# The output map of a SwiGLU feed-forward in three float32r passes, turned to token-major with one Strassen level

## The chip, the cores and the metric

The kernel runs on one core of one Trainium2 chip. The metric is the device time of one execution in microseconds, the median of three runs. The traces come from the hardware profiler.

## What is computed

One layer of a streaming encoder over 1024 prompt tokens and 64 sample tokens, 1024 channels wide: a mixer (stick-breaking attention, spatial gating and cross-attention in parallel), then a feed-forward of 2816 inner channels. The change lies in the last line:

```python
def rmsnorm(x, g):
    y = x * lax.rsqrt(jnp.mean(x * x, axis=-1, keepdims=True) + EPS)
    return y * g

def ffn_sublayer(x, g_pre, w_ffn_in, w_ffn_out, g_post):   # w_ffn_in [1024, 5632], w_ffn_out [2816, 1024]
    a, b = jnp.split(rmsnorm(x, g_pre) @ w_ffn_in, 2, axis=-1)
    return x + rmsnorm((jax.nn.silu(a) * b) @ w_ffn_out, g_post)
```

All of it is float32.

## The kernel before, in words

**Numbers.** A float32 operand is split into two float32r tiles, hi (a rounded copy, by ACT or by a CAST on DVE) and lo (source minus hi, a TENSOR_TENSOR on DVE); `split` chooses the engine of hi with `lighter`, which compares estimated clocks. A product is three passes, hi·hi, hi·lo and lo·hi (`mm3`).

**Layout.** Activations lie transposed, channels on partitions; the 1088 tokens are two halves of 544, each of sub-blocks of 288 and 256 columns. `ffn_in_unit` computes 128 inner channels with one Strassen–Winograd level (`strassen_unit`), applies silu and the gate, and stores the rows to DRAM, `actS[f]`, of which there are 22.

**The feed-forward output.** `fout_pair` calls `conv_pair` for a group of 6, 6, 5 or 5 channel blocks (`FGROUPS`) and two column tiles of 128 output channels: the weights (`whl`) are the stationary operand, the activations (`acth`, `actl`, loaded and split once by `load_act`) move, 288 or 256 columns a matmul. That is the ordinary product: 22 blocks of the contraction, 8 column tiles, three passes, 1088 columns. The sums of the groups are added up in `yacc`. The last group runs in three column groups of 512, 320 and 256 tokens (`GROUPS`), so that one group's tail runs beside the next one's products.

**The tail.** `ffn_tail` squares the rows on ACT (`ysq`), sums them over partitions with a ones-matmul, takes 1 / rms by a pow on GpSimd, transposes the 128x128 fp32 blocks back to tokens on TensorE (`pt<-ident,yacc`), and `post_stages` scales and adds the residual (SCALAR_TENSOR_TENSOR `o<-pt,rst,x2r`) before the store.

**Order.** Python emits the instructions. `run` takes the steps of products in order; `get_wop` makes weight operands `LA` steps ahead and loads `RA` further; everything else stands in streams of stages that `fill` and `breathe` take when the estimated clocks say so. Each engine then runs its own queue in that order. Loads and stores all go through SP's queue.

All instructions are recorded by one helper, so every row of the trace has line 73 (L73); tiles tell them apart.

Of the kernel before, what the change touches and what calls it, by code (L numbers as in the profile page):

```python
# [28 lines left out]
FGROUPS = [6, 6, 5, 5]  # L29
# [19 lines left out]
LA_END = 4  # L49
LA_BR = 4  # L50
# [8 lines left out]
# estimates of instructions, in us, which only order the emission: fixed part, per element of a partition  # L59
# [3 lines left out]
class Engine:  # L63
    """An engine of nc that also advances the estimated clocks."""
# [18 lines left out]
class Clocks:  # L83
    """Estimated time at which each engine has done what was emitted, and at which tiles are written and read."""
# [60 lines left out]
def encoder_layer(  # L145
# [125 lines left out]
    x2sc = [dtile([P, D], f"x2sc{t}") for t in range(9)]  # L271
    actS = [dtile([P, T], f"actS{f}") for f in range(22)]
# [45 lines left out]
    def ready(t):  # L318
        """the first stream whose next stage can start by t, or the one that can start first before t"""
# [17 lines left out]
    def breathe():  # L337
        """background stages that can start, between two short runs of products"""
# [7 lines left out]
    def fill(t):  # L346
        """background stages while products wait until t"""
# [48 lines left out]
    def wop(fn, *rs):  # L396
        """an operand made by fn from the raws rs"""
# [17 lines left out]
    def raw_load(srcs, nk):  # L415
        """srcs: one [nk*128, 256] block, or two of [nk*128, 128]"""
# [21 lines left out]
    # column ranges of the sub-blocks inside a two-bank PSUM tile; together they are contiguous  # L438
# [157 lines left out]
    def tile_rows(i):  # L596
        """token runs of token tile i: tiles 2j, 2j+1 hold the same columns of the two halves; tile 8 both rests"""
# [15 lines left out]
    def nrows(i):  # L613
        return P if i < 8 else 64
# [229 lines left out]
    def transposed(c, fin):  # L844
        """c: [128 ch, T] -> token-major [128, 9, 128]; block 8 holds the sample tokens on partitions 64.."""
# [73 lines left out]
    def load_o(b, t, s, gate=lambda: True):  # L919
        """streams that load and split the operands of branch b from the rows of the half t, sub-block s"""  # L920
# [82 lines left out]
    def post_stages(i, cols_y, rst, res_load, d, gate):  # L1003
        """d["o"] = row tile i scaled by rst(), plus the residual d["x"]; cols_y(): column blocks of its transpose"""
# [21 lines left out]
    def tile_cols(Y, i, c, pad_n=2):  # L1026
        """columns of token tile i, and their tiles, inside the tiles Y[q] ([P, 8 / len(Y), 2, n], first column c of each half)"""
# [9 lines left out]
    def row_stats(tiles, sq, c, R):  # L1037
        """1 / rms of the token tiles, one column each, from the sums sq of squares ([P, 2, n]) per partition, into R"""
# [27 lines left out]
    def mix_tail(js, Y, sq, c):  # L1066
# [4 lines left out]
        for n, i in enumerate(tiles):  # L1071
# [5 lines left out]
            def keep_x2(i=i, d=d):  # L1077
                later(0, lambda o=d["o"]: store(x2sc[i][:nrows(i)], o), [d["o"]])
# [52 lines left out]
    def ffn_in_unit(f, phases):  # L1131
# [14 lines left out]
    ACT = {}  # L1146

    def load_act(f, gate=lambda: True):
        d = {}

        def ld():
            d["r"] = A([P, T], F32, "actr")
            load(d["r"], actS[f])

        def sp():
            hi, lo = A([P, T], F32R, "acth"), A([P, T], F32R, "actl")
            split(d.pop("r"), hi, lo)
            ACT[f] = (hi, lo)
        stream(("sync", lambda: 0 if gate() else None, ld), ("act", lambda: at(d["r"]), sp))

    f0 = 0
    fgs = []
    for ng in FGROUPS:
        fgs.append(list(range(f0, f0 + ng)))
        f0 += ng

    def fout_pair(gi, p, g):
        fs = fgs[gi]
        n0 = (len(fs) + 1) // 2
# [12 lines left out]
        def evac(m_, hi, pt):
            m = 2 * p + m_
            if g is None:
                if gi == 0 and hi == 0:
# [665 lines left out]
```

## Time and profile before

| | before |
|---|---|
| median of 3 runs | 2359.42 us (2359.52, 2355.78, 2359.42) |
| the profiled execution, its own time | 2359.5 us |
| span in that profile | 2359.5 us |
| feed-forward output, first matmul to the end | 2066.2 to 2359.5 us |
| PE, DVE, ACT, POOL busy | 96%, 66%, 32%, 7% |
| matmul instructions | 17,531 |

PE is TensorE, PEld its weight loads, DVE VectorE, ACT ScalarE, POOL GpSimd, SP the engine whose queue issues the transfers. A row of the timeline has a start, a duration, engine, line, operation, tiles (out<-in) and shape; two or more operations of one kind in a row share a row (x2), and square brackets give the idle time before it and what ended it. A matmul row's duration contains its passage through the array, so the time that one takes from its neighbours is read from start to start. PEclk or the granted clock is a share of 2.4 GHz.

### The profile page before, as it was taken

The numbers are of one execution on the slowest core, as the hardware profiler recorded it, in microseconds if no ns is written. First come the engines' busy times: TensorE is split into PE (matmuls) and PEld (weight loads), VectorE is DVE, ScalarE is ACT, GpSimd is POOL, SyncE is SP. The second block draws the span as 40 slices with busy tenths as digits, with TensorE's granted clock in tenths as the row PEclk, the third lists the DMA queues.
The fourth block names the chain that finished last, engine by engine and source line by source line (L and its number), as shares of the span: only waits on it lengthen the run. The fifth ranks groups of instructions, "written<-read, shape, count | busy, mean of one in ns | idle before, by whom it ended". The sixth has DMA issues, their size and how long they took to land.

```text
span 2359.5 us, 42390 instructions
## 1 busy us (share of the span) xinstructions
PE 2270.7 (96%) x17531; PEld 2231.4 (95%) x17531; DVE 1559.2 (66%) x2408; ACT 752.6 (32%) x1325; POOL 154.2 (7%) x246
## 2 busy tenths in 40 slices
PE   7899999999999999988899999988999999999998
PEld 6799999999999998877899999988999999999997
DVE  7856688867786665799824345397667666743357
ACT  8432223232222224776512122343111211221223
POOL 1000000000000000334100000220000000000012
PEclk9999999999999999999999999998999999999998
DMA  6532356755583237754435342332222222432235
GB/s 202 179 102 99 123 206 218 237 185 179 197 269 111 93 131 269 275 194 159 141 120 159 106 155 82 123 110 64 65 74 83 83 77 62 142 120 83 93 113 172
DMA packets 239700, 333.50 MB, mean 141 GB/s; under 512 B 12100, under 2 KB 195988, under 8 KB 239508
## 3 DMA queue, kind: packets, MB, share of 16 engines
q1 hardware_dynamic: 239508, 330.78, 41.9%
q8 instruction: 139, 2.28, 0.4%
q14 instruction: 53, 0.43, 0.1%
HBM read 218.60 MB, written 112.13 MB: 140 GB/s over the span
## 4 chain that ended last, share of the span: by engine, by line
PE 47%; DVE 3%; issue 1%; DMA 0%; ACT 0%; POOLq 0%; POOL 0%; DVEq 0%; ACTq 0%
PE pb L73 46%; PE pt L73 1%; DVE whl L73 1%; DVE bt L73 0%; DMA raw<-in_w_ffn_out_dram 0%; DVE o L73 0%; DVE XhT2a L73 0%; DVE t L73 0%; DVE XhT2b L73 0%; DVE XlT3a L73 0%; DVE XlB11a L73 0%; DVE yacc L73 0%; DVE u L73 0%; DVE XhT1a L73 0%; DVE XlT2a L73 0%
## 5 line engine op out<-in xcount | busy, mean ns | idle before, releaser
L73 ACT ACTIVATE whl<-raw 128x512 fp32r<-128x512 f32 (+2 forms) x319 | 186.9, 604 | 513.0 <-PE pb L73 174.5
L73 DVE TENSOR_TENSOR c<-pb,u 128x544 f32<-128x544 f32 (+2 forms) x236 | 168.3, 713 | 246.1 <-PE pb L73 233.7
L73 PE MATMUL pb<-acth,whl 128*128 128x256 f32 (+3 forms) x1328 | 267.1, 298 | 0.6 <-DVE whl L73 0.4
L73 DVE TENSOR_TENSOR whl<-raw,whl 128x512 fp32r<-128x512 f32 (+1 forms) x382 | 239.6, 645 | 12.1 <-ACT whl L73 9.3
L73 PEld LDWEIGHTS pb<-acth,whl 128*128 128x128 f32 x1328 | 214.3, 190 | 4.9 <-DVE whl L73 1.4
L73 PE MATMUL pb<-actl,whl 128*128 128x256 f32 (+3 forms) x664 | 197.4, 297 | 0.0
L73 DVE TENSOR_TENSOR u<-pb,u 128x544 f32<-128x544 f32 (+2 forms) x177 | 125.8, 711 | 85.6 <-PE pb L73 85.6
L73 DVE TENSOR_TENSOR whl<-u,whl 128x512 fp32r<-128x512 f32 x232 | 160.0, 690 | 6.0
L73 PE MATMUL pb<-XhB11a,whl 128*128 128x288 f32 x656 | 145.0, 297 | 1.2 <-ACT whl L73 1.0
L73 PE MATMUL pb<-XhB21a,whl 128*128 128x288 f32 x656 | 145.0, 297 | 0.0
L73 PE MATMUL pb<-XhB22a,whl 128*128 128x288 f32 x656 | 144.2, 295 | 0.0
L73 PE MATMUL pb<-XhB11b,whl 128*128 128x256 f32 x656 | 132.7, 285 | 0.0
L73 PE MATMUL pb<-XhB21b,whl 128*128 128x256 f32 x656 | 131.6, 284 | 0.0
L73 PE MATMUL pb<-XhB22b,whl 128*128 128x256 f32 x656 | 131.1, 283 | 0.0
L73 PEld LDWEIGHTS pb<-actl,whl 128*128 128x128 f32 x664 | 126.5, 190 | 1.7
L73 ACT ACTIVATE c<-c 128x1088 f32<-128x1088 f32 x38 | 42.4, 1115 | 263.2 <-DVE c L73 263.2
L73 PEld LDWEIGHTS pb<-XhB11a,whl 128*128 128x128 f32 x656 | 109.8, 188 | 1.6 <-ACT whl L73 1.2
L73 PEld LDWEIGHTS pb<-XhB22a,whl 128*128 128x128 f32 x656 | 109.8, 188 | 0.0
L73 PEld LDWEIGHTS pb<-XhB21a,whl 128*128 128x128 f32 x656 | 109.8, 188 | 0.0
L73 PE MATMUL pb<-Xrh,whl 128*128 128x288 f32 (+1 forms) x512 | 102.1, 295 | 6.9 <-DVE whl L73 6.9
L73 PEld LDWEIGHTS pb<-XhB11b,whl 128*128 128x128 f32 x656 | 108.2, 192 | 0.1
L73 PEld LDWEIGHTS pb<-XhB22b,whl 128*128 128x128 f32 x656 | 107.6, 191 | 0.0
(306 smaller groups left out, 6416.3 us busy)
## 6 DMA issues: line engine op xcount, KB each, us to landing
raw<-in_w_in_dram SPq DMA_DIRECT2D x72, 512.0 KB
raw<-in_w_ffn_in_dram SPq DMA_DIRECT2D x88, 256.0 KB
gsc<-c SPq DMA_DIRECT2D x24, 544.0 KB
grow<-gsc SPq DMA_DIRECT2D x24, 544.0 KB
raw<-in_w_branch_dram SPq DMA_DIRECT2D x24, 512.0 KB
raw<-in_w_ffn_out_dram SPq DMA_DIRECT2D x32, 384.0 KB
actS<-c SPq DMA_DIRECT2D x22, 544.0 KB
actr<-actS SPq DMA_DIRECT2D x22, 544.0 KB
```

Source lines behind the costliest of these rows:

```text
L73: r = fn(*a, **k)
```

## The change

The output map is computed token-major: the split activations (`fop`, 128 channels by 128 tokens) are stationary, and 512 columns of the split weights move. One Strassen–Winograd level goes over the halves of the contraction (11 blocks each), of the 1024 prompt tokens and of the 1024 output columns. Seven products p1, p2, p6, p7, p5, p3, p4 in that order take 11 steps each; a step is one channel block, with 2 token pairs (`jp`) of 2 tiles, 3 passes, 12 matmuls of 512 columns.

- **Operands** (`fout_ops`). Weight tiles `fw` of 128x512 are loaded for each product anew. p6 loads three, makes T1 = B12 - B11 on GpSimd (`psub`) and T2 = B22 - T1 on DVE and stores both to DRAM (`tS`), from which p5 and p4 load them again. p7's difference of weights is on DVE, p4's on GpSimd. Activations are loaded as `fa`, 44 half rows, from the last units of ffn_in on (`fout_load`, `FA_GATE`), and stay; the sums S1 are made on GpSimd (`padd`), the differences on DVE (p6) or GpSimd (p7, p3). Each operand is then split.
- **Sample tokens** (64) ride in p1, p2, p5 and p3 as two more matmuls a step whose stationary operand holds hi and lo side by side (`fs`); two fp32 matmuls with `sel` add the halves at the end. They are the ordinary product.
- **Sums of products** (`fout_post`): two-bank PSUM tiles of 128x1024 go into `t1`, `C11`, `U3`, `C22` in SBUF, by ACT or DVE. `scaled` squares with a running sum on ACT (no ones-matmul, no transposes) and multiplies by the gain: on GpSimd for C11 and C22, on DVE else.
- **p4** runs first its 11 steps for the first two token tiles only and keeps the operands (`first`), then the other two tiles one after the other with nothing to make (`rest`).
- **End:** `square` takes 1 / rms by token and one SCALAR_TENSOR_TENSOR a half row adds the residual, then half rows are stored, 18 in all.
- Lookahead in the stage: `LA_END` 4 operands as before, `RA_END` 2 for loads. Ahead of the stage, `x2sc` is stored by token, and each of the 22 units stores its 64 sample columns apart (32 KB more on SP's queue).

```diff
-ACT = {}
-def load_act(f, ...): ...
-def fout_pair(gi, p, g): ...        # conv_pair over FGROUPS, yacc, ysq
-def ffn_tail(js, sq, c): ...        # row_stats, transposes, post_stages
...
+            def put():
+                store(actS[f], c[0][:, :1024])
+                store(sS[f // 11][:, f % 11], c[0][:, 1024:])
+                STORED.add(f)
...
+    def fout_ops(name, k):
+        B = {"11": lambda: w_raw(k, 0), "12": lambda: w_raw(k, 512), "21": lambda: w_raw(NK + k, 0),
+             "22": lambda: w_raw(NK + k, 512)}
+        r = [x() for x in {"p1": [B["11"]], "p2": [B["21"]], "p6": [B["12"], B["11"], B["22"]],
+                           "p7": [B["22"], B["12"]], "p5": [lambda: t_raw(0, k)], "p3": [B["22"]],
+                           "p4": [B["21"], lambda: t_raw(1, k)]}[name]]
+        def w():
+            x = [get_raw(i) for i in r]
+            if name == "p6":
+                psub(x[0], x[0], x[1])
+                sub(x[2], x[2], x[0])
+                later(0, lambda: store(tS[0][k], x[0]), [x[0]])
+                later(0, lambda: store(tS[1][k], x[2]), [x[2]])
+                return fsplit(x[2])
+            if name == "p7":
+                sub(x[0], x[0], x[1])
+            elif name == "p4":
+                psub(x[0], x[0], x[1])
+            return fsplit(x[0])
+        def a():
...
+            if name in ("p1", "p2", "p4", "p5"):
+                return fsplit(src(*{"p1": (0, 0), "p2": (0, 1), "p4": (1, 1), "p5": (1, 0)}[name]))
+            if name == "p6":
+                until(lambda: ("s1", k // 2) in FO)
+                x = src(0, 0)
+                sub(x, src(1, 0), x)
+                return fsplit(x)
+            if name == "p7":
+                x = U([P, 512], F32, "fs3")
+                psub(x, src(1, 1), src(0, 0))
+                return fsplit(x)
+            x = src(0, 1)
+            psub(x, x, src(0, 0))
+            return fsplit(x)
+        return wop(w, *r), wop(a)
...
+    def fout_mm(pt, a, w, jp, js, k):
+        for j in js:
+            mm3(pt[:, (j % 2) * 512:(j % 2) * 512 + 512], a[:, 0, j * P:(j + 1) * P], a[:, 1, j * P:(j + 1) * P],
+                w[:, 0], w[:, 1], k == 0, k == NK - 1)
...
+    def scaled(j0, m, c, eng):
+        for i in range(2):
+            square(j0 + i, m, c[:, i])
+        g = FO["g"][:, m * 512:(m + 1) * 512]
+        for i in range(2):
+            eng(c[:, i], c[:, i], g)
...
+    def fout_post(name, jp, pt):
...
+        if name == "p1":
+            act(new("t1"), src)
+        elif name == "p2":
+            c = new("C11")
+            add(c, src, FO["t1", jp])
+            scaled(2 * jp, 0, c, pmul)
+        elif name == "p6":
+            t = FO["t1", jp]
+            add(t, src, t)
+        elif name == "p7":
+            add(new("U3"), src, FO["t1", jp])
+        elif name == "p5":
+            c = new("C22")
+            add(c, src, FO["U3", jp])
+            t = FO["t1", jp]
+            add(t, src, t)
+            scaled(4 + 2 * jp, 1, c, pmul)
+        elif name == "p3":
+            t = FO.pop(("t1", jp))
+            add(t, src, t)
+            scaled(2 * jp, 1, t, mul)
...
-    for n, f in enumerate(fgs[0]):
-        load_act(f, lambda n=n: pos[0] > p1 + n)
+    fout_load(p1)
     run(7)
     LA[0] = LA_END
-    drain()
+    RA[0] = RA_END
+    fout_begin()
     run(n_fout)
     drain()
```

Two places in the order of the instructions. The first is GpSimd's queue where p2 ends and p6 begins. Before, it held at the end of the program the last sums of squares (`ysq`):

```order
L73 TENSOR_TENSOR ysq_24784<-ysq_24784,ysq_24812 128x512
L73 TENSOR_TENSOR ysq_24784<-ysq_24784,ysq_24841 128x512
L73 TENSOR_TENSOR ysq_24784<-ysq_24784,ysq_24870 128x512
L73 TENSOR_TENSOR ysq_24784<-ysq_24784,ysq_24899 128x512
```

Now (`fa` a sum S1, `fw` the weight differences of p6's steps, `C_` the gain products of C11):

```order
L73 TENSOR_TENSOR fa_22895<-fa_22895,fa_22765 128x1024
L73 TENSOR_TENSOR fw_23258<-fw_23258,fw_23260 128x512
L73 TENSOR_TENSOR fw_23284<-fw_23284,fw_23286 128x512
L73 TENSOR_TENSOR C_3075_23336<-C_3075_23336,gpf_22800 128x512 x2
L73 TENSOR_TENSOR C_3080_23354<-C_3080_23354,gpf_22800 128x512 x2
L73 TENSOR_TENSOR fw_23315<-fw_23315,fw_23317 128x512
L73 TENSOR_TENSOR fw_23368<-fw_23368,fw_23370 128x512
```

The differences of steps 0 and 1 stand ahead of the four products, that of step 2 behind them.

The second is DVE's queue in the same place. Before, in the early part of the stage, it held one lo of 384 columns for several matmuls, and copies into `yacc`:

```order
L73 COPY yacc_22867<-pb_22869 128x544
L73 TENSOR_TENSOR whl_22911<-raw_22738,whl_22911 128x384
L73 TENSOR_TENSOR whl_22916<-raw_22820,whl_22916 128x384
L73 TENSOR_TENSOR actl_22932<-actr_22929,acth_22931 128x1088
L73 COPY yacc_22962<-pb_22919 128x544
```

Now, from C11's additions to the operands of p6's step 2 (`pb` is a PSUM tile of products, `t_` is t1, `ys` the sample rows):

```order
L73 TENSOR_TENSOR C_3075_23336<-pb_23087,t_3030_23065 128x1024
L73 TENSOR_TENSOR C_3080_23354<-pb_23094,t_3031_23073 128x1024
L73 TENSOR_TENSOR ys_3085_23366<-pt_23101,ys_23077 128x512
L73 TENSOR_TENSOR fw_23319<-fw_23319,fw_23315 128x512
L73 CAST fop_23376<-fw_23319 128x512
L73 TENSOR_TENSOR fop_23376<-fw_23319,fop_23376 128x512
L73 TENSOR_TENSOR fa_22526<-fa_22870,fa_22526 128x512
L73 CAST fop_23380<-fa_22526 128x512
```

All operations of an operand of p6 stand on DVE, its first behind a GpSimd difference (`fw_23315`).

## Rows read from the trace of the kernel before

**Rows 1.** From the page: the span; busy time and instructions of PE, and the granted clock in 40 equal slices (tenths).

```profile
span 2359.5 us, 42390 instructions
...
PE 2270.7 (96%) x17531; PEld 2231.4 (95%) x17531; DVE 1559.2 (66%) x2408; ACT 752.6 (32%) x1325; POOL 154.2 (7%) x246
...
PEclk9999999999999999999999999998999999999998
```

**Rows 2.** The tile `acth` on PE, hi activations of the feed-forward output: minimum, median and maximum duration in ns, first and last start, forms.

```profile
L73 PE MATMUL pb<-acth,whl x1328: 274/293/562, 2066.2 to 2348.0; 128*128 128x256 f32 x89, 128*128 128x288 f32 x78, 128*128 128x320 f32 x12, 128*128 128x512 f32 x11
```

**Rows 3.** Stretches: length, then busy us and instructions of PE, PEld, DVE, ACT, POOL, granted clock, DMA share, GB/s. The first lies at the end of ffn_in, the others in the feed-forward output.

```profile
2050.00:2060.00 10.00, 10.00 (x82) 10.00 (x82) 8.44 (x13) 4.51 (x6) 0.00 (x0) 1.00 1.00 365
2100.00:2150.00 50.00, 50.00 (x400) 50.00 (x399) 17.65 (x27) 9.97 (x16) 0.00 (x0) 1.00 0.28 90
2310.00:2320.00 10.00, 10.00 (x73) 9.73 (x72) 9.36 (x18) 4.55 (x11) 2.91 (x3) 1.00 0.91 317
```

**Rows 4.** Timeline of PE: two of the matmuls of 512 columns, 39 starts apart, and further on eight fp32 transposes and the matmul behind them.

```profile
2289.99 0.40 PE L73 MATMUL pb<-actl,whl 128*128 128x512 f32 x1
...
2299.05 0.40 PE L73 MATMUL pb<-actl,whl 128*128 128x512 f32 x1
...
2306.12 1.04 PE L73 MATMUL pt<-ident,yacc 128*128 128x128 f32 x8
2306.91 0.40 PE L73 MATMUL pb<-acth,whl 128*128 128x320 f32 x1
```

**Rows 5.** Groups of equal instructions, shapes apart: count, busy us, mean ns of one, idle time before them. The first five over the whole program, the last two over the stretch from 2066 on.

```profile
L73 DVE TENSOR_TENSOR whl<-raw,whl 128x512 fp32r<-128x512 f32 x286 | 193.2, 690 | 8.5 <-ACT whl L73 7.4
L73 ACT ACTIVATE whl<-raw 128x512 fp32r<-128x512 f32 x254 | 157.1, 634 | 419.6 <-DMA raw<-in_w_in_dram 127.9 <-PE pb L73 109.9 <-DMA raw<-in_w_ffn_in_dram 66.5
L73 POOL TENSOR_TENSOR rstd<-rstd,mhalf 128x1 f32<-128x1 f32 x26 | 19.2, 738 | 389.6 <-DVE rstd L73 389.6
L73 DVE SCALAR_TENSOR_TENSOR o<-pt,rst,x2r 128x512 f32<-128x512 f32 x16 | 11.4, 745 | 2.1 <-PE pt L73 1.1 <-POOL rst L73 0.8
L73 DVE TENSOR_TENSOR ptl<-pb,pth 128x1024 fp32r<-128x1024 f32 x8 | 9.8, 1224 | 10.6 <-ACT pth L73 10.6
...
L73 POOL TENSOR_TENSOR ysq<-ysq,ysq 128x512 f32<-128x512 f32 x5 | 7.1, 1411 | 680.2 <-ACT ysq L73 680.2
L73 ACT ACTIVATE ysq<-yacc 128x512 f32<-128x512 f32 x8 | 5.1, 632 | 24.1 <-DVE yacc L73 24.1
```

**Rows 6.** Timeline of DVE near the end of ffn_in: a subtraction, the CAST and the lo that depend on it, and an independent operation.

```profile
2049.72 0.68 DVE L73 TENSOR_TENSOR u<-raw 128x512 f32<-128x512 f32 x1
2050.44 0.43 DVE L73 CAST whl<-u 128x512 fp32r<-128x512 f32 x1
2050.90 0.69 DVE L73 TENSOR_TENSOR whl<-u,whl 128x512 fp32r<-128x512 f32 x1
2051.51 0.72 DVE L73 TENSOR_TENSOR c<-pb,u 128x544 f32<-128x544 f32 x1
```

**Rows 7.** Timeline of POOL from 1548 to 1566 us, in an earlier stage.

```profile
1548.42 1.56 POOL L73 TENSOR_TENSOR ysum<-ysum,ysq 128x512 f32<-128x512 f32 x1 [3.40 <-ACT ysq L73]
1553.53 1.82 POOL L73 TENSOR_TENSOR bt<-bt 128x512 f32<-128x512 f32 x1 [3.55 <-DVE bt L73]
1557.10 1.73 POOL L73 TENSOR_TENSOR bt<-bt 128x512 f32<-128x512 f32 x1 [1.76 <-DVE bt L73]
...
1564.36 1.61 POOL L73 TENSOR_TENSOR ysum<-ysum,ysq 128x512 f32<-128x512 f32 x1 [1.12 <-ACT ysq L73]
```

**Rows 8.** Timeline of DVE in the same stretch.

```profile
1548.88 1.65 DVE L73 TENSOR_TENSOR whl<-raw,whl 128x512 fp32r<-128x512 f32 x1
...
1553.50 0.69 DVE L73 TENSOR_TENSOR t<-bt,bt 128x512 f32<-128x512 f32 x1
1554.22 1.40 DVE L73 CAST XhT2a<-t 128x512 fp32r<-128x512 f32 x1
...
1557.72 1.40 DVE L73 CAST XhT2a<-t 128x512 fp32r<-128x512 f32 x1
...
1560.36 0.42 DVE L73 CAST XhT1a<-bt 128x512 fp32r<-128x512 f32 x1
...
1564.16 2.35 DVE L73 TENSOR_TENSOR XlT3a<-bt,XhT3a 128x512 fp32r<-128x512 f32 x2
1566.44 1.28 DVE L73 TENSOR_TENSOR XlB22a<-bt,XhB22a 128x512 fp32r<-128x512 f32 x2
```

**Rows 9.** Timeline of single instructions: the store of a unit's rows on SP's queue (SPq), the last matmul of the products, and the last two residual steps.

```profile
2047.32 0.34 SPq L73 DMA_DIRECT2D actS<-c  x1
...
2347.96 0.28 PE L73 MATMUL pb<-acth,whl 128*128 128x256 f32 x1
...
2353.37 1.60 DVE L73 SCALAR_TENSOR_TENSOR o<-pt,rst,x2r 128x512 f32<-128x512 f32 x2 [0.55 <-PE pt L73]
```

**Rows 10.** Stretches, columns as in rows 3: one from the attention stage, three from the end of the feed-forward output.

```profile
1108.00:1112.00 4.00, 2.52 (x22) 2.29 (x21) 3.90 (x5) 3.31 (x7) 3.33 (x5) 1.00 0.99 391
2341.00:2342.00 1.00, 0.04 (x1) 0.04 (x1) 1.00 (x3) 0.69 (x2) 0.17 (x1) 0.54 0.83 193
2342.00:2343.00 1.00, 1.00 (x5) 1.00 (x6) 0.56 (x1) 0.23 (x1) 0.57 (x1) 0.50 0.01 0
2347.00:2348.00 1.00, 1.00 (x7) 1.00 (x6) 0.00 (x0) 0.00 (x0) 0.00 (x0) 0.55 0.97 303
```

More of the change, by code (lines that the diff above doesn't have):

```diff
@@ L32 @@
 G_BIAS = 1
-G2_BIAS = 9
 PE_COL = 0.000417
-PADD = [6, 6, 6]
 LA_FIRST = 2
@@ new lines, in fout_begin, with w_raw, f, t_raw @@
+    def fout_begin():
+        sel = FO["sel"] = U([P, 2, 64], F32, "sel")
+        for i in range(2):
+            add(sel[:, i], ident[:, :64], ident[:, 64:])
+    def w_raw(k, c, n=512):
+        def f():
+            r = U([P, n], F32, "fw")
+            load(r, w_ffn_out[0, k * P:(k + 1) * P, c:c + n])
+            return r
+        raws.append(f)
+        return len(raws) - 1
+    def t_raw(i, k):
+        def f():
+            r = U([P, 512], F32, "fw")
+            load(r, tS[i][k])
+            return r
+        raws.append(f)
+        return len(raws) - 1
@@ new lines, in sample_out, with do @@
+    def sample_out():
+        def do():
+            y = [FO["y1"], FO["y"][:, 1]]
+            pt = PB()
+            for i in range(2):
+                nc.tensor.matmul(pt[:, i * 512:(i + 1) * 512], lhsT=FO["sel"].rearrange("p i n -> p (i n)"), rhs=y[i],
+                                 start=True, stop=True)
+            c = A([P, 2, 512], F32, "yc")
+            act(c[:64], pt[:64].rearrange("p (i n) -> p i n", i=2))
+            for i in range(2):
+                square(8, i, c[:64, i])
+                mul(c[:64, i], c[:64, i], FO["g"][:64, i * 512:(i + 1) * 512])
+        stream(("pe", lambda: max(at(FO["y"], FO["y1"]), psum_free("b")), do))
@@ new lines, in encoder_layer, with square, ld, put @@
+    SQ, RES = {}, {}
+    def square(j, m, src):
+        n = src.shape[0]
+        ss = sm.tile([P, 1], F32, tag="ssf", name=nm("ssf"), bufs=18)[:n]
+        act(U([P, 512], F32, "junk")[:n], src, AF.Square, accum_out=ss)
+        SQ.setdefault(j, {})[m] = (ss, src)
+        if len(SQ[j]) == 2:
+            s0, s1 = SQ[j][0][0], SQ[j][1][0]
+            add(s0, s0, s1)
+            SQ[j]["r"] = rstd_of(s0, D)
+            n_ = n
+            def ld():
+                x = RES[j] = A([P, D], F32, "x2r")[:n_]
+                load(x, x2sc[j * P:j * P + n_])
+            def put(m):
+                src = SQ[j][m][1]
+                x = RES[j][:, m * 512:(m + 1) * 512]
+                nc.vector.scalar_tensor_tensor(x, src, SQ[j]["r"], x, op0=ALU.mult, op1=ALU.add)
+            def out(m):
+                x = RES[j][:, m * 512:(m + 1) * 512]
+                store(y_prompt[0][j * P:(j + 1) * P, m * 512:(m + 1) * 512] if j < 8 else
+                      y_sample[0][:, m * 512:(m + 1) * 512], x)
+            need = ("dve", lambda: max(at(RES[j], SQ[j]["r"]), at(SQ[j][0][1], SQ[j][1][1])))
+            st = [x for m in range(2) for x in ((*need, lambda m=m: put(m)),
+                                                ("sync", lambda: at(RES[j]), lambda m=m: out(m)))]
+            if j in RES:
+                stream(*st)
+            else:
+                stream(("sync", lambda: 0, ld), *st)
@@ new lines, in res_early, with pmul, pair, new @@
+    def res_early(j):
+        x = RES[j] = A([P, D], F32, "x2r")
+        load(x, x2sc[j * P:j * P + P])
+    def scaled(j0, m, c, eng):
+        for i in range(2):
+            square(j0 + i, m, c[:, i])
+        g = FO["g"][:, m * 512:(m + 1) * 512]
+        for i in range(2):
+            eng(c[:, i], c[:, i], g)
+    def pmul(out, a, b):
+        nc.gpsimd.tensor_tensor(out, a, b, op=ALU.mult)
+    def pair(pt):
+        return pt.rearrange("p (i n) -> p i n", i=2)
+    def fout_post(name, jp, pt):
+        def new(key):
+            FO[key, jp] = A([P, 2, 512], F32, key)
+            return FO[key, jp]
+        src = pair(pt)
+        if name == "p1":
+            act(new("t1"), src)
+        elif name == "p2":
+            c = new("C11")
[16 more added lines that the diff above has]
+            scaled(2 * jp, 1, t, mul)
@@ new lines, in last_tile, with fout_step, f @@
+    def last_tile(j, pt):
+        u = FO["U3", j // 2][:, j % 2]
+        add(u, pt[:, (j % 2) * 512:(j % 2) * 512 + 512], u)
+        square(4 + j, 0, u)
+        mul(u, u, FO["g"][:, :512])
+    def fout_step(name, k):
+        ws = fout_ops(name, k)
+        def f(tiles):
+            w, a = tiles
+            if name == "p1" and k == 0:
+                FO["g"] = A([P, D], F32, "gpf")
+                load(FO["g"], g_post_ffn.to_broadcast([P, D]))
+            for jp in range(2):
+                if k == 0:
+                    fill(psum_free("b"))
+                    FO["pt", jp] = PB()
+                pt = FO["pt", jp]
+                fill(at(w, a))
+                fout_mm(pt, a, w, jp, (2 * jp, 2 * jp + 1), k)
+                if k == NK - 1:
+                    fout_post(name, jp, pt)
+                breathe()
+            if name in SAMPLE:
+                until(lambda: ("s", SAMPLE[name][0]) in FO)
+                fout_sample(name, w, k)
+        steps.append((ws, f))
@@ new lines, in fout_last, with first, f, rest @@
+    def fout_last():
+        kept = []
+        def first(k, ws):
+            def f(tiles):
+                w, a = tiles
+                kept.append((w, a))
+                if k == 0:
+                    fill(psum_free("b"))
+                    FO["pt", 0] = PB()
+                fill(at(w, a))
+                fout_mm(FO["pt", 0], a, w, 0, (0, 1), k)
+                breathe()
+                if k == NK - 1:
+                    for j in range(2):
+                        last_tile(j, FO["pt", 0])
+            steps.append((ws, f))
+        def rest(j):
+            def f(tiles):
+                if j == 2:
+                    fill(psum_free("b"))
+                    FO["pt", 1] = PB()
+                res_early(4 + j)
+                for k, (w, a) in enumerate(kept):
+                    fout_mm(FO["pt", 1], a, w, 1, (j,), k)
+                    if k % 3 == 2:
+                        breathe()
+                last_tile(j, FO["pt", 1])
+            steps.append(([], f))
+        for k in range(NK):
+            first(k, fout_ops("p4", k))
+        for j in (2, 3):
+            rest(j)
@@ L1245, in encoder_layer @@
+    for name in ("p1", "p2", "p6", "p7", "p5", "p3"):
+        for k in range(NK):
+            fout_step(name, k)
+    fout_last()
     n_fout = len(steps) - n_mem - n_win - n_branch - n_out - n_fin
```

183 lines of the change are left out of this document (86 added, 97 removed).

## The prediction, before the changed kernel was run

> **What bounds the kernel now.** I read the page first, then the tiles' view of the changed stage, its stretches, and last the single rows of TensorE, VectorE and GpSimd. On the page [rows 1] the reader is to see PE busy 96% of the span under a clock that is full nearly throughout. The tiles' view [rows 2] places the feed-forward output: its first matmul starts at 2066.2, its last at 2348.0, so with the span's end at 2359.5 the stage takes 293.3 us, and everything ahead of 2066.2 runs the same matmuls in the same order in both kernels. The stretches [rows 3] show this stage PE-paced: 50.00 of 50 us with vector work at 17.65 and DMA at 0.28. So here columns are time. The opposite is to be seen just before it (2050 to 2060: vector work 8.44 of 10, DMA share 1.00 at 365 GB/s) and near its end (2310 to 2320: VectorE 9.36 of 10, DMA 0.91 at 317). The profiled execution reports 2359.5 us, which is also the run of 2359.52, 0.1 over the median of 2359.42; the runs spread by 3.7 us, and about 0.2% (4.7 us) is what a measurement tells from no change.
>
> **What goes.** 1992 matmuls of 574,464 columns. Of 512 columns, counted from one lo matmul's start to another's, 39 take 2299.05 - 2289.99 = 9.06 us, 0.2323 each [rows 4]. Matmuls of 288 and 256, 272 in the mean, take 50/400 = 0.125 [rows 3], so per column it is 0.454 and 0.460 ns: width buys little, the columns must fall. With them go the transposes, the ones-matmul and the vector additions of the old tail.
>
> **What comes: PE's floor.** 1012 matmuls of 512 (518,144 columns) and two fp32 ones. p1, p2, p5, p3 have 14 matmuls in each of 11 steps: 14 x 0.2323 = 3.25 a step, 35.8 each, 143.1 together. p6, p7 and p4 have 12: 2.79 a step, 30.7 each, 92.0. The fp32 pair I take as the eight fp32 transposes that move 1024 columns, 0.79 from start to start of the next matmul up to 1.04 [rows 4]: 0.9. Floor 236.0. After the last matmul: addition of a PSUM tile half, 0.7; square 0.63; two small steps, 0.4; pow 0.74; two residual steps 2 x 0.745 [rows 5]; then from the last residual step's end (2353.37 + 1.60 = 2354.97) to 2359.5 it is 4.5 in the old tail [rows 9], kept. Together 8.5, with handovers 9. The old tail was 11.3 [rows 9]. Without any wait the end would be 2066.2 + 236.0 + 9 = 2311.2, 48 us earlier. The question is what PE waits for.
>
> **Costs of operand making.** Formerly one split served 17 or 5 blocks of columns; now every 12 or 14 matmuls need two fresh operands, each a rounding (hi) and a subtraction (lo), and the sums of the scheme besides. On VectorE a subtraction that feeds a CAST costs 0.72 until the CAST starts, the CAST 0.46, and an independent one follows 0.61 later [rows 6]; on ACT a hi is 0.63 [rows 5]. The GpSimd sums are 1.41 each [rows 5].
>
> **GpSimd holds VectorE.** Set GpSimd's rows [rows 7] against VectorE's [rows 8]: TENSOR_TENSOR whl at 1548.88, which is 0.69 alone, takes 1.65 and ends as the GpSimd addition started at 1548.42 ends; CASTs at 1554.22 and 1557.72 take 1.40 beside the additions of 1553.53 and 1557.10, against 0.42 at 1560.36; the pair at 1564.16 takes 2.35 against 1.28 for the pair at 1566.44. Each loses 0.95 to 1.1. I take 1.0 us for each GpSimd operation that meets a CAST or a two-input operation in SBUF. Whether an operation meets one is the uncertain thing: one that started first is not held (1553.50).
>
> **Phase by phase, what PE waits beyond the floor.**
> p1 and p2: 6. On SP's queue the 44 half-row activation loads (256 KB each), two sample loads (352 KB), the gains (512 KB), two units' stores (1.1 MB) and eight weight tiles make 15.95 MB up to the weights of step 7. The queue is free from 2047.32 + 0.34 [rows 9]; at 365 GB/s [rows 3] this lands at 2091.4. Step 7 begins at 2066.2 + 7 x 3.25 = 2089.0 and wants it 2 us before for the split: 4.4 late (at 317 GB/s, 11). The GpSimd sums of activations (5 of 1024 and one of 512 columns, 11 x 1.41 = 15.5) lie under p2; their holds cost 1.6.
> p6: 19. Four gain products of C11 stand on GpSimd's queue before the weight difference of step 2. They wait for ACT's squares: the first pair's PSUM tile ends 1.9 before p2's end, its addition takes 1.22 and a square 0.63 [rows 5], so with handovers the products start 0.4 after p2's end: 0.4 + 5 x 1.41 = 7.4 until the difference is there, then 3.6 on VectorE (two differences, two CASTs, two lo's) and a hold: 12 against 5.6 for which steps 0 and 1 last, 6 lost. From there each step takes VectorE 3.58 + about 0.8 of hold = 4.4 against 2.79: eight steps, 13. The two extra stores and three loads a step are 1.31 MB, 3.6 to 4.1 us at 365 to 317 GB/s, under 4.4.
> p7: 6. A step is 2.40 + 1.0 = 3.4 against 2.79: nine, 5.5, and 0.5 at its start, where a PSUM buffer waits for p6's addition (1.22 [rows 5]).
> p5: 0. One load and 1.2 of VectorE a step; PE's 3.25 covers it. If that load came late it would cost up to p1's 4.4.
> p3: 5. Four gain products of C22 stand before the difference of step 2 (7.4 again, then a split, against 6.5): 3, and 2 of holds.
> p4: 21. Its first part has 6 matmuls a step, 15.3 in all, 16.2 with the fp32 pair. VectorE has there: two additions 2.4, sample 0.7, four gain products 2.4, eleven pairs of lo's 11 x 1.22 = 13.4, eight residual steps 8 x 0.745 = 6.0: 25.0. About 5.6 it stands behind the chain addition, square, four pows of 0.74 on GpSimd's queue, difference; about 6 of the 15 GpSimd operations hold it: 37.0. The second part, 66 matmuls on operands kept, waits for nothing.
> Clock: 2.5. Where PE stood for nearly a microsecond (2341 to 2342) the granted clock was 0.54, and it was 0.50 to 0.55, the 1.2 GHz level, to the last matmul at 2348 [rows 10]; I take some 5 us of it, which lose half; PE idles like that through p4's first part, and the second begins so. At a PE share of 2.52 in 4 us, with short gaps, the clock stayed 1.00 [rows 10], so p6 keeps it.
> Earlier: 0. 22 more stores of 32 KB, 0.34 each on SP [rows 9], lie under ffn_in, where PE leads; uncovered, 7.5.
> Sum: 6 + 19 + 6 + 5 + 20.8 + 2.5 = 59.3, so 2311.2 + 59.3 = **2370.5**, 11 over the profiled time: slower by 0.5%.
>
> **The rivals.**
> R1, faster: GpSimd's operations fall into VectorE's gaps and hold nothing (one in four above did not). Waits 2 + 11.7 + 3 + 2 + 14.4 + 2.5 = 35.6: 2346.8. It turns at 0.54 us of hold an operation, (48.3 - 35.6)/(59.3 - 35.6). Against it: VectorE is the pace there and hardly has gaps. For it: in p6 the difference for two steps on can run while the vector engine adds from PSUM.
> R2, same: only CASTs are held, not the two-input subtractions (most of the held rows are CASTs). 4.5 + 16 + 3 + 2.5 + 17.6 + 2.5 = 46.1: 2357.3. Against it the rows at 1548.88 and 1564.16.
> R3, much slower: GpSimd's queued operations hold VectorE back to back, and loads come at 317 GB/s: 12.5 + 21 + 8 + 13 + 23 + 2.5 = 80: 2391.2.
> R4, same: the matmuls start closer. The 512-column rows move two runs of 256; the new ones move one run. At one column in a 2.4 GHz cycle they would take 0.2133, and the phases that PE paces (p1, p2, p5, p3 and p4's second part, 158 us) would lose 0.019/0.2323 = 8%, 13 us: 2357.5. Against it: 0.46 and 0.454 ns a column over two widths.
> R4 is what the Trainium skill has ("TensorE: Matmul & The Clock Gate", Back-to-back issue gap): columns over 2.4 GHz plus 2.5 ns, 216 ns for 512. By that figure 158 us would shrink by 11, to an estimated 2359.3; the rows at 0.2323 do not agree.
> Against R1 and R2 speaks a rule of the Trainium skill ("GPSIMD Engine Reference", Key points): GpSimd contends with vector instructions that have two SBUF inputs or a two-port mode, and these rows agree: 1.65 against 0.69 and 1.40 against 0.42.
>
> **Chances.** Forecast 0.45, R1 0.25 (no trace shows how the holds fall here), R2 0.12, R3 0.13, R4 0.05. Faster 0.25, same R2 + R4 = 0.17, slower 0.58. The range goes from R1 to R3 with 1.9, half the runs' spread, beyond each: 2344.9 to 2393.1; the forecast alone 2360 to 2377, from holds of 0.55 and from loads 6.6 later than taken.
>
> **What would show it.** In p6: VectorE near full, PE about 63%, CASTs or lo's of 1.4 to 1.8 us beside GpSimd's differences; a first p6 gap of some 6 us. DMA share 1.00 from 2048 to 2092 with a wait near step 7. p4's first part at 37 us. p5 at 35.8. Half clock after it. A tail of 9. I am wrong if p6 lasts 42 or less (R1), if matmuls start 0.215 apart (R4), or if PE waits for DMA in p6.

## The result, and the profile after

The changed kernel takes 2385.48 us (2383.04 to 2386.0, four runs), the kernel before beside it 2357.6: ratio 1.0118, interval 1.0104 to 1.0133. It is 27.9 us slower where 11 were forecast; the range of the prediction held it. The profiled execution of the changed kernel took 2385.9 us by its own time and its span is 2383.8; the traces are compared by span, 24.3 us over [rows 1].

The page after: span, PE, and the costliest group of the new matmuls (busy us, mean ns | idle time before them and what ended it).

```profile
span 2383.8 us, 40664 instructions
...
PE 2247.1 (94%) x16465; PEld 2154.2 (90%) x16465; DVE 1639.1 (69%) x2471; ACT 746.7 (31%) x1324; POOL 233.6 (10%) x294
...
L73 PE MATMUL pb<-fop,fop 128*128 128x512 f32 x924 | 245.1, 416 | 44.9 <-DVE fop L73 36.2
```

PE works 23.6 us less than before and still ends later: it waits for `fop` operands (the split tiles of weights and activations). Where these matmuls lie, from the tiles' view (answers to [rows 2]):

```profile
L73 PE MATMUL pb<-fop,fop x924: 387/389/796, 2067.2 to 2376.1; 128*128 128x512 f32 x185
```

From 2067.2 to the span's end are 316.6 us, 293.3 before. How close matmuls follow each other, from PE's timeline in p2, where nothing waits (answers to [rows 4]):

```profile
2127.00 2.88 PE L73 MATMUL pb<-fop,fop 128*128 128x512 f32 x12
2129.72 0.61 PE L73 MATMUL pt<-fop,fs 128*128 128x512 f32 x2
2130.18 0.62 PE L73 MATMUL pb<-fop,fop 128*128 128x512 f32 x2
```

A step of 14 takes 2130.18 - 2127.00 = 3.18; over the eleven steps of p2 it is 34.9/154 = 0.2267 a matmul, not 0.2323. The floor is 1012 x 0.2267 = 229.4. The lengths of the phases, from the start of one's first matmul to that of the next one's, and what each has over its matmuls at 0.2267 (p4's forecast is its 20.8 and the 0.9 of the fp32 pair, which lies in its length):

| | p1 | p2 | p6 | p7 | p5 | p3 | p4, first part | second | tail |
|---|---|---|---|---|---|---|---|---|---|
| length, us | 53.5 | 34.9 | 51.7 | 39.7 | 34.9 | 41.6 | 36.8 | 16.1 | 7.5 |
| over the floor | 18.6 | 0 | 21.8 | 9.8 | 0 | 6.7 | 21.8 | 1.1 | |
| forecast | 6 (with p2) | | 19 | 6 | 0 | 5 | 21.7 | 2.5 | 9 |

Stretches of the changed kernel, columns as in [rows 3]: p1, p2, the end of p1's loads, the steady part of p6, p4's first part.

```profile
2067.20:2120.70 53.50, 41.85 (x157) 31.24 (x156) 35.49 (x47) 11.90 (x22) 15.74 (x7) 0.87 0.81 276
2120.70:2155.60 34.90, 34.90 (x156) 28.91 (x155) 18.21 (x29) 7.96 (x14) 1.29 (x1) 1.00 0.27 90
2096.00:2106.00 10.00, 4.36 (x9) 2.79 (x10) 9.93 (x5) 5.00 (x11) 9.40 (x4) 0.55 0.92 340
2172.00:2192.00 20.00, 15.20 (x58) 9.93 (x58) 19.10 (x28) 0.00 (x0) 5.93 (x4) 1.00 0.84 290
2336.00:2346.00 10.00, 5.52 (x16) 3.78 (x15) 9.97 (x10) 5.94 (x12) 5.89 (x5) 0.83 0.34 105
```

In p1 the granted clock is 0.87 in the mean and the DMA share 0.81; p2, with the same work, waits for nothing. DVE's timeline in p1, idle time in brackets:

```profile
2078.27 0.43 DVE L73 CAST fop<-fw 128x512 fp32r<-128x512 f32 x1 [5.15 <-DMA fw<-in_w_ffn_out_dram]
...
2095.30 2.34 DVE L73 CAST fop<-fw 128x512 fp32r<-128x512 f32 x1 [5.05 <-DMA fw<-in_w_ffn_out_dram]
2097.68 2.71 DVE L73 TENSOR_TENSOR fop<-fw,fop 128x512 fp32r<-128x512 f32 x1
2100.31 2.84 DVE L73 TENSOR_TENSOR fop<-fa,fop 128x512 fp32r<-128x512 f32 x1
2103.07 2.61 DVE L73 CAST fop<-fw 128x512 fp32r<-128x512 f32 x1
```

and POOL's, here and in later phases:

```profile
2092.71 12.69 POOL L73 TENSOR_TENSOR fa<-fa,fa 128x1024 f32<-128x1024 f32 x5 [0.57 <-DMA fa<-actS]
...
2156.07 5.05 POOL L73 TENSOR_TENSOR C<-C,gpf 128x512 f32<-128x512 f32 x4 [30.93 <-ACT junk L73]
2161.08 2.48 POOL L73 TENSOR_TENSOR fw<-fw,fw 128x512 f32<-128x512 f32 x2
...
2218.31 1.67 POOL L73 TENSOR_TENSOR fs<-fa,fa 128x512 f32<-128x512 f32 x1 [1.81 <-DVE fop L73]
...
2339.30 4.98 POOL L73 TENSOR_TENSOR fw<-fw,fw 128x512 f32<-128x512 f32 x4
```

First weight tiles come late (5.2 us for one step, 5.1 for another); then, beside GpSimd's 1024-column sums, each vector operation takes 2.3 to 2.8 us instead of 0.43 or 0.69. These four take 10.5 us instead of 2.2, 8.3 more. Counted from 0 and over the floor of 3.17, steps 0 to 2 of p1 lose 6.3 us, step 5 4.6, step 6 7.0, the others 0.7 together. DVE in p6 (two rows), p7 and p4:

```profile
2162.37 1.73 DVE L73 TENSOR_TENSOR fw<-fw,fw 128x512 f32<-128x512 f32 x1 [5.24 <-POOL fw L73]
...
2178.65 1.31 DVE L73 CAST fop<-fa 128x512 fp32r<-128x512 f32 x1
...
2218.75 1.78 DVE L73 TENSOR_TENSOR fw<-fw,fw 128x512 f32<-128x512 f32 x1
...
2338.84 7.32 DVE L73 SCALAR_TENSOR_TENSOR x2r<-C,rstd,x2r 128x512 f32<-128x512 f32 x3
```

The first shows p6's gap: GpSimd has to get through four gain products first. The next two are holds of about 1.0 us, as in [rows 8]. The last is new: three residual steps of 0.75 take 7.32 beside four differences; one by one the first takes 5.99, the other two 0.73 each.

p7's start is a wait of another kind. The waits of PE from 2155 to 2250, and DVE:

```profile
PE pb L73 <- DVE t L73: 3.1, 1, 3.1
...
2210.62 2.35 DVE L73 TENSOR_TENSOR t<-pb,t 128x1024 f32<-128x1024 f32 x2
```

PE needs a PSUM buffer that p6's last additions (`t`) have not yet emptied; they stand on VectorE's queue behind the operands of a step of p7. The first two steps of p7 lose 5.0 of its 9.8 us, with the lower clock behind the wait.

The end, PE and DVE:

```profile
2375.65 0.84 PE L73 MATMUL pb<-fop,fop 128*128 128x512 f32 x3
...
2380.06 0.74 DVE L73 SCALAR_TENSOR_TENSOR x2r<-C,rstd,x2r 128x512 f32<-128x512 f32 x1
```

From the last residual step to the end are 3.0 us, against 4.5 in [rows 9].

### The profile page after: what moved, and what is told of

Its sections match the earlier page's. It is cut to its first block, busy times and chain, and to the rows that moved or that the text cites. A ratio compares the mean times of both kernels' runs of the same rounds, so it can differ in the third digit from the quotient of the medians.

```text
span 2383.8 us, 40664 instructions
## 1 busy us (share of the span) xinstructions
PE 2247.1 (94%) x16465; PEld 2154.2 (90%) x16465; DVE 1639.1 (69%) x2471; ACT 746.7 (31%) x1324; POOL 233.6 (10%) x294
## 4 chain that ended last, share of the span: by engine, by line
PE 40%; DVE 6%; DMA 2%; issue 2%; POOL 1%; SPq 0%; ACT 0%; POOLq 0%; DVEq 0%; ACTq 0%
PE pb L73 39%; DVE fop L73 2%; PE pt L73 2%; DMA fa<-actS 1%; DVE fw L73 1%; DVE bt L73 1%; POOL C L73 0%; DVE t L73 0%; DMA raw<-in_w_ffn_in_dram 0%; DVE x2r L73 0%; DVE fa L73 0%; DMA actS<-c 0%; SPq L73 0%; DMA fw<-in_w_ffn_out_dram 0%; POOL fw L73 0%
## 5 line engine op out<-in xcount | busy, mean ns | idle before, releaser
L73 ACT ACTIVATE whl<-raw 128x512 fp32r<-128x512 f32 x254 | 157.0, 633 | 440.6 <-DMA raw<-in_w_in_dram 135.3
L73 PE MATMUL pb<-fop,fop 128*128 128x512 f32 x924 | 245.1, 416 | 44.9 <-DVE fop L73 36.2
L73 PEld LDWEIGHTS pb<-fop,fop 128*128 128x128 f32 x924 | 182.0, 200 | 101.4 <-DVE fop L73 46.2
L73 DVE TENSOR_TENSOR whl<-raw,whl 128x512 fp32r<-128x512 f32 x286 | 193.1, 689 | 13.7 <-ACT whl L73 12.6
L73 PEld LDWEIGHTS pb<-XhB21b,whl 128*128 128x128 f32 x656 | 107.5, 191 | 0.0
L73 PE MATMUL pb<-XhT1a,whl 128*128 128x288 f32 x464 | 102.1, 296 | 0.6 <-DVE sgo L73 0.6
```

The costliest lines, as they stand in the source:

```text
L73: r = fn(*a, **k)
```

## The experiments

Theory: p1 waits for weight tiles that stand behind activation loads; p6, p7 and p4 are VectorE's pace, stretched by GpSimd's holds; GpSimd's queue order makes the gaps at the start of p6 and p3. Rivals: holds alone for p1, or SP's chain of stores and loads for p6. A hold is time by which a vector operation takes longer beside GpSimd's. Lengths of the phases in us in one profiled execution each, as above, and medians:

| kernel | p1 | p2 | p6 | p7 | p5 | p3 | p4 first | second | median | ratio to before |
|---|---|---|---|---|---|---|---|---|---|---|
| changed | 53.5 | 34.9 | 51.7 | 39.7 | 34.9 | 41.6 | 36.8 | 16.1 | 2385.5 | 1.0118 |
| loads spread | 35.3 | 37.5 | 51.9 | 40.5 | 34.9 | 41.5 | 38.1 | 16.1 | 2370.9 | 1.0049 (1.0034 to 1.0064) |
| hi's on ACT | 49.3 | 34.9 | 52.4 | 42.2 | 34.9 | 38.2 | 38.0 | 16.1 | 2382.0 | 1.0102 (1.0084 to 1.0119) |
| no GpSimd | 45.4 | 34.9 | 47.8 | 41.7 | 34.9 | 36.1 | 36.1 | 16.1 | 2369.1 | 1.0042 (1.0027 to 1.0057) |
| gains later | 52.0 | 34.9 | 45.7 | 46.4 | 37.1 | 34.9 | 38.4 | 16.1 | 2379.2 | 1.0085 (1.0068 to 1.0102) |
| residuals late | 50.4 | 34.9 | 52.2 | 40.6 | 34.9 | 41.5 | 34.2 | 20.2 | 2385.5 | 1.0118 (1.0103 to 1.0133) |
| two runs | 50.9 | 35.6 | 51.8 | 40.7 | 35.6 | 42.2 | 36.7 | 16.5 | 2385.9 | 1.0118 (1.0098 to 1.0139) |
| p6 order | 52.5 | 34.9 | 48.1 | 40.4 | 34.9 | 38.9 | 36.6 | 16.1 | 2376.7 | 1.0078 (1.0061 to 1.0094) |
| combined | 35.5 | 34.9 | 37.5 | 36.7 | 34.9 | 34.9 | 34.6 | 16.1 | 2340.6 | 0.9925 (0.9911 to 0.9940) |
| combined, 2nd | 35.5 | 34.9 | 33.9 | 37.2 | 34.9 | 34.9 | 32.2 | 16.1 | 2333.4 | 0.9899 (0.9882 to 0.9915) |

p1 varies between 49.3 and 53.5 in kernels that leave its loads and sums alone, so less than 4 us there says nothing.

**Loads spread.**

```diff
-FA_GATE = [1, 1, 2, 2, 3, 3, 4, 4, 4, 5, 5, 6, 6, 6, 7, 7, 8, 8, 9, 9, 10, 10, 2, 9]
+FA_GATE = [1, 1, 2, 2, 3, 4, 5, 6, 7, 9, 10, 11, 12, 13, 14, 15, 16, 17, 18, 19, 20, 21, 2, 12]
```

> The changed kernel with the half-row activation loads spread out: the second contraction half is loaded from p1's middle on, the second token half and its sums S1 during p2 (only the gates' numbers change). Theory, loads: p1's waits (53.5 us against a floor of 34.9) come from weight tiles that stand behind activation loads on the queue. Then p1 falls to about 38, p2 grows by at most 3 (GpSimd's sums now fall there, one a step), and the whole from 2385.5 to about 2371. Rival, holds: the waits are those of vector operations held by GpSimd's five 1024-column sums; they only move: p1 about 45, p2 about 43, the whole 2383 or more.

p1 is at its floor of 34.9 within 0.4, p2 2.6 longer, the whole 14.6 shorter. p1 and p2 of this kernel:

```profile
2066.40:2101.70 35.30, 35.26 (x156) 28.85 (x155) 26.08 (x39) 9.88 (x19) 5.83 (x3) 1.00 0.92 332
2101.70:2139.20 37.50, 35.46 (x156) 28.68 (x155) 31.42 (x39) 8.00 (x14) 12.15 (x6) 1.00 0.47 155
```

DMA is as busy in p1 as before, and PE waits for next to none of it: with the loads in this order the wait is gone. But the run moves the sums S1 along with the loads. Their 13.1 us of 1024-column operations now run from 2097.2 on, 8.6 of them in p2, and hold five vector operations again, to 2.6 to 2.9 us each; with operands made ahead this costs PE at most 2.6. So holds alone don't explain p1, and what they took in it, where the operands were late already, the run without GpSimd has to tell.

**Hi's on ACT.** In `fsplit`:

```diff
-        split(src, t[:, 0], t[:, 1])
+        act(t[:, 0], src)
+        sub(t[:, 1], src, f32(t[:, 0]))
```

> The changed kernel with every hi of a fop operand on ScalarE instead of the engine that the estimate chooses. Theory, VectorE paces p6 and p7: without two CASTs p6's step falls from 4.53 to about 3.65 us and p7's from 3.49 to about 3.0; p6 51.7 to about 43, p7 39.7 to about 35, the whole 2385.5 to about 2373. Rival, the chain of loads and stores on SP's queue (two stores, three loads a step, also 4.5 us) paces p6: p6 stays at 50 or more and the whole gains 4 or less.

The forecast failed: p6 52.4, p7 42.2, both no shorter. DVE in p6:

```profile
2172.02 0.69 DVE L73 TENSOR_TENSOR fop<-fw,fop 128x512 fp32r<-128x512 f32 x1 [0.70 <-ACT fop L73]
...
2175.17 0.69 DVE L73 TENSOR_TENSOR fop<-fa,fop 128x512 fp32r<-128x512 f32 x1 [0.78 <-ACT fop L73]
```

VectorE stands 0.7 to 0.8 us before each lo, longer than the CAST that it saved (0.46). So the rival's numbers came (p6 over 50, 3.5 us gained) without showing the rival; the next one tells.

**p6 order**, on top of the last: the difference of activations is issued before the split of the weights.

```diff
             if name == "p6":
...
+                y = fo_src((0, 0), k)
+                sub(y, fo_src((1, 0), k), y)
                 return fsplit(x[2])
...
-                x = src(0, 0)
-                sub(x, src(1, 0), x)
-                return fsplit(x)
+                return fsplit(src(0, 0))
```

> The kernel with every hi on ScalarE (the second experiment, 2382.0), and in p6 both differences of a step issued on VectorE ahead of its two lo's. Theory: that experiment gained little because VectorE waited in order for ScalarE's hi between difference and lo, twice a step; now the second difference covers the first hi, and p6's step falls from about 4.7 to about 3.7, p6 from 52.4 to about 44, the whole from 2382.0 to about 2374. Rival, stores and loads on SP's queue pace p6: p6 stays at 50 or more.

p6 is 48.1, half of the way. DVE and then POOL of this kernel:

```profile
2173.20 0.69 DVE L73 TENSOR_TENSOR fop<-fw,fop 128x512 fp32r<-128x512 f32 x1
...
2176.66 0.69 DVE L73 TENSOR_TENSOR fw<-fw,fw 128x512 f32<-128x512 f32 x1 [2.08 <-POOL fw L73]
...
2175.33 1.29 POOL L73 TENSOR_TENSOR fw<-fw,fw 128x512 f32<-128x512 f32 x1 [3.98 <-DMA fw<-in_w_ffn_out_dram]
```

The waits for ACT are down to 0.15 us or less, and the next one stands there: GpSimd's difference waits for the load. Both theories hold part of p6: VectorE paced it, and the transfers are close behind.

**No GpSimd.** `psub`, `padd` and `pmul` of the stage become `sub`, `add` and `mul` on VectorE.

> The changed kernel with all 512- and 1024-column sums, differences and gain products of the stage on VectorE, GpSimd keeps only the pows. Theory, holds: a difference on GpSimd costs VectorE 1.0 us or more, one on VectorE 0.61. p6's step 4.53 to about 4.2, p7's 3.49 to about 3.0, p3's waits 6.7 to about 2, p1's by 5 less, p4's first part about even; the whole 2385.5 to about 2368. Rival, holds cost nothing much beyond what the trace shows as longer operations and VectorE's added work counts: every step of p6, p7 and p4 gets 0.6 longer and the whole is 2395 or more.

The total is as forecast, not all of its parts: p3 -5.5, p6 -3.9, p1 -8.1 (up to 4 of it within its variation), p7 +2.0, where the hi of the activations, on ACT before, became a CAST. DVE, and stretches of p1 and p6:

```profile
2161.28 1.41 DVE L73 TENSOR_TENSOR fw<-fw,fw 128x512 f32<-128x512 f32 x2
...
2067.00:2112.00 45.00, 39.97 (x154) 30.58 (x153) 27.78 (x44) 11.53 (x22) 0.00 (x0) 0.92 0.86 307
2160.00:2180.00 20.00, 15.65 (x60) 10.34 (x59) 18.93 (x33) 0.00 (x0) 0.00 (x0) 0.99 0.88 292
```

VectorE took over all of GpSimd's sums, differences and products, and the whole got 16 us shorter. A difference given away cost VectorE a little more than one done: p6's step falls from 4.53 to 4.38. The larger gains have other reasons: in p3 and at p6's start GpSimd's queue order (next run), in p1 the holds of the sums. With the loads as they were and no holds, p1 still has 10.4 us over its floor, most of it at steps 1 and 2 (6.1).

**Gains later.** In `scaled` the gain products of C11 and C22 go; four each come as `mul` in p5's steps 3 to 6 and p3's 5 to 8.

> The changed kernel with the eight gain products of C11 and C22 taken off GpSimd's queue and done on VectorE later, where it is half idle (in p5's steps 3 to 6 and p3's 5 to 8). Theory, GpSimd's queue: they delay the difference for step 2 of p6 and of p3. Then p6's gap of 5.4 us before step 2 falls below 1.5, p3's waits from 6.7 to about 4 (eight differences still hold VectorE), the whole 2385.5 to about 2378. Rival: step 2 waits for its own chain (loads, difference, two splits): the gap stays above 4, the whole within 2 us.

The gap before p6's step 2 is gone (step 3 comes 0.9 us late), and p3 waits for nothing, as the queue's theory said. But p7 and p5 get 8.9 longer. POOL and then DVE at p7's end:

```profile
2230.39 16.36 POOL L73 TENSOR_TENSOR fa<-fa,fa 128x512 f32<-128x512 f32 x10
...
2234.39 1.40 DVE L73 CAST fop<-fw 128x512 fp32r<-128x512 f32 x1
2235.83 1.64 DVE L73 TENSOR_TENSOR fop<-fw,fop 128x512 fp32r<-128x512 f32 x1
```

Freed of the gain products, GpSimd runs ten differences of p3 early, and holds p7 instead: part of the cost moved.

**Residuals late.** `need` of the residual steps returns None until p4's second part.

> The changed kernel with the residual steps of the finished tiles (eight of the prompt, two of the sample) held back until p4's second part. Theory, VectorE paces p4's first part: ten steps of 0.75 us, which GpSimd's differences hold up to 2.4 us each there, leave it, so it falls from 36.75 to about 28 us; the second part has VectorE free and grows by 2 at most, the tail by 2; the whole 2385.5 to about 2380. Rival, the loads of weights and of the stored differences pace it (GpSimd waited 7.7 us for one): the first part stays at 34 or more and the whole does not gain, or loses by the later stores.

The first part gains 2.6 and the second loses 4.1; in all nothing. POOL and then DVE in the first part:

```profile
2335.35 0.93 POOL L73 TENSOR_TENSOR rstd<-rstd,mhalf 64x1 f32<-64x1 f32 x1 [4.49 <-DMA fw<-tS]
2336.25 7.41 POOL L73 TENSOR_TENSOR fw<-fw,fw 128x512 f32<-128x512 f32 x6
...
2337.57 6.38 DVE L73 CAST fop<-fw 128x512 fp32r<-128x512 f32 x1 [1.70 <-POOL fw L73]
```

The rival's numbers came, and part of its reason: GpSimd waited 4.5 us for a stored difference. But then it ran six differences in a row, and one CAST of 0.43 was held until the last of them ended.

**Two runs.** Each `fop` operand lies as two runs of 256 columns, 16 apart.

```diff
-        t = A([P, 2, 512], F32R, "fop")
+        t = A([P, 2, 2, 272], F32R, "fop")[:, :, :, :256]
```

> The changed kernel with each 512-column operand laid out as two runs of 256 columns with a gap of 16, as the 512-column matmuls of the kernel before had it. Theory: the second run is what made those matmuls start 0.2323 us apart instead of the changed kernel's 0.2267; then p2's steps go from 3.17 back to 3.25 us and the floor grows by 5.7. Rival, the layout of the moving operand makes no difference (the stationary tile or something else does): p2's steps stay at 3.17.

PE in p2 of this kernel:

```profile
2121.55 2.93 PE L73 MATMUL pb<-fop,fop 128*128 128x512 f32 x12
...
2124.78 2.93 PE L73 MATMUL pb<-fop,fop 128*128 128x512 f32 x12
```

3.23 for 14 matmuls, 0.2310 each. The second run costs 0.0043 of the 0.0056 us between the two kernels; the rest stays open. The median didn't move; p1, which varies, was 2.6 shorter in this profile.

**Combined.** Loads spread, no GpSimd but for the pows, hi's on ACT with a step's differences first, p6's difference of activations moved to p2, gains later.

> A version meant to beat both: loads spread as in the first experiment, all sums and differences on VectorE, hi's on ScalarE with the differences of a step issued first, p6's difference of activations moved into p2, the gain products of C11 and C22 in p5 and p3. If loads, holds and VectorE's load are what p1, p6, p7 and p3 wait for, they come to about 36, 33, 33 and 35 us, p2 36, p5 35, p4 as now, and the whole to about 2335. If SP's chain of loads and stores paces p6 (4.5 us a step), p6 stays near 48 and the whole comes to about 2350.

It beats both kernels. p6 in the middle:

```profile
2145.00:2165.00 20.00, 17.35 (x68) 11.95 (x66) 14.42 (x23) 6.79 (x12) 0.00 (x0) 1.00 0.98 344
```

VectorE has room now and the DMA share is 0.98: five transfers of 256 KB are 1.31 MB, 3.8 us at 344 GB/s, against 3.7 in the mean of p6's five steps there.

**Combined, 2nd.** T1 is made again in p5 instead of stored in p6; the last statistics and gain products stand behind the next operands.

```diff
-                           "p7": [B["22"], B["12"]], "p5": [lambda: t_raw(0, k)], "p3": [B["22"]],
+                           "p7": [B["22"], B["12"]], "p5": [B["12"], B["11"]], "p3": [B["22"]],
...
-                later(0, lambda: store(tS[0][k], x[0]), [x[0]])
```

> The combined version (2340.6) with two more edits. p6 no longer stores T1; p5 loads B12 and B11 and subtracts again, on VectorE, which is half idle there. Theory: with holds and queue order gone, p6 is paced by its DMA (five transfers of 256 KB a step at a share of 0.97 to 0.99), so its step falls with the bytes, from 3.8 to about 3.1 us, and p6 from 37.5 to about 32; p5 stays at 35. And the sums, the pow and the gain products of the last tiles are issued behind the next operands instead of ahead of them: p4's gap of 6.0 us before step 2 falls to about 3, its first part from 34.6 to about 31. The whole from 2340.6 to about 2332. Rival, VectorE's own chain with ScalarE paces p6: p6 stays at 36 or more; and p4's first part is VectorE's sum of work, whatever the order: it stays at 34.

p6 33.9 and p4's first part 32.2: both went the way expected, by about two thirds of the forecast; p4's gap before step 2 is still 5.6 us. At 2333.4 us it is 1.0% faster than the kernel before. Over the floor it keeps 17.3 us in p4's first part (the fp32 pair is in it), 7.2 in p7, all of it in the first two steps, and 3.9 in p6; nothing here tried p7's start.

## Why the prediction was wrong in size

The direction held, and VectorE, GpSimd and p4's sum were where the time went. The sum 2066.2 + 236.0 + 9 + 59.3 became 2067.2 + 229.4 + 7.5 + 79.7 (the fp32 pair now within p4): waits were 20 us longer than forecast, the matmuls themselves shorter. Point by point:

- **p1: the step that failed.** 6 us were forecast for p1 and p2, 18.6 came in p1 alone. The prediction asked when the whole backlog would be through, and compared that with step 7 alone, as if the steps before it ran on time. But from step 1 on each weight tile stood behind up to ten activation tiles: steps 0 to 2 lost 6.3 us before any sum ran, and VectorE stood idle for 5.15 and 5.05 us for two tiles. Without GpSimd 10.4 us remained; with the loads spread, and the sums with them, 0.4 did. The rate, 318 GB/s from 2067.2 to 2107 and not 365, made it worse: by the prediction's own sum 11 instead of 4.4 at step 7.
- **The sums S1: nearly the other half of it.** They were to lie under p2 and cost 1.6. They fell under p1's steps 5 and 6, and held four vector operations of 0.43 and 0.69 to 2.3 to 2.8 us each, 8.3 in sum; taking them off GpSimd made p1 8.1 shorter, at least 3.9 of it beyond p1's variation. 1.0 was the price beside a 512-column operation; beside a 1024-column one it is about 2. They cost this much because the operands were late already: in the run with the loads spread the same holds cost 2.6 at most.
- **p6** 21.8 against 19, by the mechanism given: a gap of 5.4 (forecast 6) and steps of 4.5 to 4.8 (4.4), VectorE 19.10 of 20 us busy.
- **p7** 9.8 against 6, and otherwise made up. VectorE's step was right (1.78 for a held 0.69, 3.49 in all), but operands made ahead covered it up to step 6, so that it cost 2 us and not 5.5. The wait for p6's additions at its start, priced at 0.5, cost 5.0. And GpSimd runs ahead to p3's differences near p7's end, where step 8 loses 2.8.
- **p3, p4**: 6.7 against 5, and 36.8 against 37.0 (the terms written there add up to 36.6). In p4 the size was right by luck, for the split wasn't: a hold runs to 6 us, GpSimd itself waits 4.5 us for a stored difference ahead of it, and without any GpSimd difference the part still took 36.1. Which of these paces it stays open.
- **The clock** was priced once, at 2.5, where p4's second part begins; that part lost 1.1, at full clock, 0.8 of it a wait for an addition. Instead the granted clock fell to half (1.2 GHz) behind the gaps of p1, p6, p7, p3 and p4. Summed over the matmuls in those stretches, what each took over 0.2267 (up to 0.2) is 15.6 us, 3.7 of it in p1 and 5.1 in p4; it is contained in the phases' numbers, and what a full clock alone would give back wasn't tried.
- **The floor** came out 6.6 lower (5.7 in the matmuls of 512, the rest is the fp32 pair, now counted in p4), which by luck hid part of the miss: R4's direction was right, at 0.2267 and not at 0.2133, and by the two-run layout mostly. The Trainium skill ("TensorE: Matmul & The Clock Gate", Back-to-back issue gap) has 0.216 for 512 columns, as the gap of an isolated matmul, and 0.131 for a sustained stream; p2, a sustained stream at full clock, shows 0.2267 and agrees with neither.
- **The rivals.** R1 and R2 fell: a hold cost 0.9 to 1.1 us beside a 512-column operation, over R1's turning point of 0.54, and two-input operations were held like CASTs. (The whl at 1548.88, from which the price was read, ends 0.55 after the GpSimd addition and not with it; the loss of 0.96 stands.) R3 was right on mechanism: loads came at 318 GB/s, and GpSimd's queued work did hold one operation of VectorE for 6.4 us on end (residuals late). The Trainium skill ("GPSIMD Engine Reference", Key points) names the contention, and these runs price it: 0.9 to 6 us an operation held.

## What to carry to other kernels

Check a backlog of transfers at each step that needs a tile, not at its end: what is needed first must be first on the queue. Elementwise work given to GpSimd is no relief for a VectorE that sets the pace with two-input operations and CASTs in SBUF: here a difference given away cost it as much as one done, and holds cost most where operands were late already. And a gap costs PE twice, once as a wait and again as a lower granted clock behind it.

## What was not expected of the hardware

A hold is not always one operation long. Beside a run of GpSimd operations VectorE mostly advanced by one operation for each (1.4 to 1.8 us), but once stood for 6.38 us until the sixth of a row had ended, and one residual step of 0.75 took 5.99 beside four; what decides between the two wasn't settled. A moving operand in two runs of 256 columns cost 0.0043 us a matmul against one of 512.
